# Row decays by DMA instead of matmuls, two output rows finished later, and the step sizes' chain ahead of a silu, in a one-core decoder-layer kernel

## The chip, the cores and the metric

The kernel runs on one core of a Trainium2 chip. A core has five engines that run side by side, each with its own instruction stream in a fixed order: PE (TensorE, matmuls; its weight loads are listed as PEld), DVE (VectorE), ACT (ScalarE), POOL (GpSimd) and SP (which here only issues DMAs). An instruction that waits holds up everything behind it on its engine. The metric is the device time of one execution in microseconds (us). Of this kernel three runs are given, and one further execution that the hardware profiler recorded.

## What is computed

One inference step of one decoder layer, for one prompt of 2048 tokens and 32 sample tokens that share the weights: a mixer of two halves (gated linear attention "GLA" and a Mamba-2 state space "SSD"), cross-attention to a memory of 256 tokens, and a SwiGLU feed-forward of width 2816, with model width 1024. All is fp32; each large fp32 product is made of three matmuls on operands split into a high and a low part.

The part that the change touches first is the SSD half. It has 8 heads and goes in chunks of tokens. With step sizes `dt` (a softplus) and a per-head rate `a_head` the reference computes per chunk

```
lc = jnp.cumsum(dtc * a_head, axis=1)
seg = lc[:, :, None, :] - lc[:, None, :, :]
decay = jnp.exp(jnp.where(causal, seg, -jnp.inf))
cb = jnp.einsum('bthn,bshn->btsh', cc, bc)
y = (jnp.einsum('btsh,bshp->bthp', cb * decay * dtc[:, None], xc) + ...
```

so for each head and each chunk a square matrix exp(lc[t] - lc[s]) is needed. With the source token s on the partitions, lc[s] is one number per partition, and lc[t] is a row that all 128 partitions must see: the "row decays".

## The kernel before

**Phase A (0 to about 840 us)** does projections, convolution, SSD and GLA in four blocks of 512 tokens (starting near 0, 250, 430 and 610 us). A block first makes the convolution features and one narrow projection (tile `sp`: step sizes and gate ranks), applies silu to the features (`xc`, L209/L210), and then makes, in this order, z (`tm(0)`), g (`tm(1)`), q and k, and v, each as a long run of PE matmuls at L135 to L137. Beside these runs go generators that stand in a queue `side` and are stepped between projection units: `decays()` (the softplus chain L155 to L171, `dA` L629, cumulative sums `lc` by two matmuls L632/L633), `gates()` (L659 to L679), and then the SSD chunks, four of 128 tokens in a block, each as `ssd_first(c)` and `ssd_second(c)`. A scheduler puts the instructions of this phase into each engine's stream by priorities, so the streams are not in the order of the code; they are fixed when the kernel is built.

Row decays before, for every block: `lc` is split into two parts (`hl`, L641/L642), transposed by four PE instructions (L646) and copied to 16 partitions of `sp` (`lcT`, L647). For each chunk POOL multiplies these 16 rows by a mask into a tile `R` of 16 x 1024 (L775), which was zeroed once in the block (L679). Two matmuls against a matrix of ones (`onesr`, L801), 128 x 512 each, put the rows onto all 128 partitions in PSUM. DVE takes min and difference with lc[s] from PSUM into `M` (L805, eight of 128 x 128 a chunk), ACT the exponential (L806), DVE multiplies by the masked C·B product (L809, two), and PE uses `M` as weights (L819, eight matmuls).

ACT keeps one table of functions at a time: silu and exp stand in different ones, and each change is an ACT_TABLE_LOAD in its stream. The code asks for the exponentials' table after the silus of the features, of z (L728) and of g (L735, L863).

**The passes behind (840 us to the end)** are the mixer's output, the scores, the value product, the feed-forward gate/up (kind "g", three units, the first starting near 1367 us) and down. Each is a row of units of seven products in a Strassen-like scheme with twelve matmul groups; the order of the code is kept. The seven products need sums of input pieces, which ACT (L1739) and DVE (L1743) prepare from tiles `st` that SP loads (L1795); the piece makers are called `now` (this unit) and `coming` (the next pass). Finished output rows are post-processed by generators in the list `posts`, each of which `tick()` advances by one step per product: `after_rows(j, m)` scales a row block (L1830), adds the residual by DMA, sums squares (L1900), scales by the root mean square into `u` (L1906), and `turned` transposes it on PE (L1863, eight). Row blocks are numbered (j, m) with j = 0 to 7 and m = 0, 1; the last two values of j finish when the value pass has ended and the gate/up pass has begun. Only when `posts` is empty in the gate/up pass does `leave_attention()` (L2178) free the attention's tiles and start the samples' work.

## Time and profile before

| | us |
|---|---|
| three runs | 2791.37, 2798.59, 2800.58 |
| their median | 2798.59 |
| the profiled execution, its own time | 2795.36 |
| its span (first to last recorded instruction) | 2793.6 |

| engine | busy us | share of the span |
|---|---|---|
| PE | 2720.1 | 97% |
| DVE | 2075.6 | 74% |
| ACT | 1472.2 | 53% |
| POOL | 540.1 | 19% |

The profile is one execution. A view by windows gives, per stretch of time, each engine's busy time with its number of instructions, the granted clock of PE (1.00 is full speed) and the DMA's share. A view of waits gives how long an engine stood idle, for which instruction and line, and which instruction of which other engine ended that. A timeline gives start and length of single instructions, with equal neighbours drawn together. PE's matmuls are pipelined: one begins before the one ahead has ended, so what a matmul costs is the distance from its start to the next start, and not its length.

### The profile page before, as it was taken

The page shows a single profiled execution, that of the slowest core. Times are in us where ns is not written, and L with a number is a line of the kernel's source. Part 1 is how long each engine was busy: PE and PEld are TensorE (multiplying, and loading weights), DVE is VectorE, ACT ScalarE, POOL GpSimd, SP SyncE. Part 2 cuts the span into 40 slices and gives each one's busy share as a digit, 9 for nine tenths or more (in the row PEclk, how much of TensorE's full clock was granted, in tenths as well). Part 3 has the DMA queues.
Part 4 walks back from the last instruction along what each step waited for, and adds up shares of the span by engine and source line. Part 5 has one row for each costly group of instructions (what it writes and reads, how often), then busy time and mean ns, then how long its engine had stood idle before and what let it go on. Part 6 is the DMA issues. An engine that isn't in the chain of part 4 may idle for free.

```text
span 2793.6 us, 41826 instructions
## 1 busy us (share of the span) xinstructions
PE 2720.1 (97%) x15207; PEld 2362.1 (85%) x15207; DVE 2075.6 (74%) x3831; ACT 1472.2 (53%) x2921; POOL 540.1 (19%) x722
## 2 busy tenths in 40 slices
PE   8999999999999999999899999999999999999998
PEld 8988888787886888888799888899999998788886
DVE  7676677776758787777888788668678888574776
ACT  5545554544547787777755434434445555353432
POOL 2142332321321321025321210001000001000011
PEclk9999999999999999999999999999999999999999
DMA  7345435343267885468764567775235436465765
GB/s 257 114 143 190 150 103 163 121 129 95 83 193 254 284 303 216 152 200 255 260 219 179 189 239 240 255 252 179 99 138 179 152 121 211 163 218 109 240 157 130
DMA packets 151102, 512.17 MB, mean 183 GB/s; under 512 B 18176, under 2 KB 29488, under 8 KB 137328
## 3 DMA queue, kind: packets, MB, share of 16 engines
q1 hardware_dynamic: 94560, 331.81, 36.3%
q0 software_dynamic: 44240, 152.82, 16.8%
q10 hardware_dynamic: 12096, 24.86, 2.7%
q8 instruction: 120, 1.97, 0.3%
q14 instruction: 86, 0.70, 0.1%
HBM read 365.76 MB, written 143.67 MB: 182 GB/s over the span
## 4 chain that ended last, share of the span: by engine, by line
PE 78%; DVE 11%; ACT 4%; issue 3%; DMA 3%; POOL 1%; DVEq 0%; POOLq 0%; SPq 0%; ACTq 0%
PE accA L135 10%; PE accA L136 10%; PE accA L137 10%; PE accC L135 5%; PE acc L135 5%; PE accC L137 5%; PE accC L136 5%; PE acc L136 5%; PE acc L137 5%; PE accB L135 3%; PE accB L137 3%; PE accB L136 3%; DVE s L1670 2%; DVE sum L1650 1%; PE mx L1863 1%
## 5 line engine op out<-in xcount | busy, mean ns | idle before, releaser
L135 PE MATMUL accA<-r,s 128*128 128x512 f32 (+2 forms) x1792 | 636.5, 355 | 17.4 <-ACT r L1739 5.8
L137 PE MATMUL accA<-r,s 128*128 128x512 f32 (+2 forms) x1792 | 629.0, 351 | 3.3 <-DVE s L1670 3.2
L136 PE MATMUL accA<-r,s 128*128 128x384 f32 (+2 forms) x1472 | 503.1, 342 | 3.1 <-DVE r L1743 3.0
L135 PEld LDWEIGHTS accA<-r,s 128*128 128x128 f32 x1792 | 339.6, 190 | 67.2 <-issue 9.7
L1668 ACT ACTIVATE s<-sum 128x512 fp32r<-128x512 f32 (+1 forms) x456 | 282.1, 619 | 192.6 <-DVE sum L1650 89.9
L137 PEld LDWEIGHTS accA<-r,s 128*128 128x128 f32 x1792 | 339.6, 189 | 33.8 <-DVE s L1670 4.7
L1670 DVE TENSOR_TENSOR s<-sum,s 128x512 fp32r<-128x512 f32 (+1 forms) x456 | 306.5, 679 | 20.5 <-ACT s L1668 20.1
L135 PE MATMUL accC<-r,s 128*128 128x512 f32 (+2 forms) x896 | 316.9, 354 | 4.4 <-ACT sg L1977 2.8
L137 PE MATMUL accC<-r,s 128*128 128x512 f32 (+2 forms) x896 | 312.6, 349 | 0.0
L136 PEld LDWEIGHTS accA<-r,s 128*128 128x128 f32 x1472 | 279.2, 190 | 20.8 <-DVE r L1743 5.1
L1670 DVE TENSOR_TENSOR s<-raw,s 128x512 fp32r<-128x512 f32 (+1 forms) x342 | 232.8, 681 | 51.3 <-ACT s L1668 50.3
L136 PE MATMUL accC<-r,s 128*128 128x384 f32 (+2 forms) x736 | 250.0, 340 | 0.5 <-DVE r L1743 0.5
L1668 ACT ACTIVATE s<-raw 128x512 fp32r<-128x512 f32 (+1 forms) x342 | 212.8, 623 | 66.3 <-PE accC L137 48.5
L129 ACT ACTIVATE whi<-wraw 128x1024 fp32r<-128x1024 f32 (+2 forms) x140 | 128.8, 934 | 184.7 <-PE acc L136 104.6
L135 PEld LDWEIGHTS accC<-r,s 128*128 128x128 f32 x896 | 168.6, 188 | 31.6 <-ACT sg L1977 6.3
L130 DVE TENSOR_TENSOR wlo<-wraw,whi 128x1024 fp32r<-128x1024 f32 (+2 forms) x140 | 152.3, 1099 | 47.2 <-ACT whi L129 46.5
L137 PEld LDWEIGHTS accC<-r,s 128*128 128x128 f32 x896 | 168.6, 188 | 14.7 <-DVE s L1670 0.2
L143 POOL TENSOR_TENSOR rs<-ms,nhalf 128x1 f32<-128x1 f32 (+4 forms) x125 | 113.0, 906 | 345.8 <-DVE ms L141 330.8
L135 PE MATMUL acc<-xhl,whi 128*128 128x512 f32 (+1 forms) x464 | 167.5, 362 | 8.4 <-ACT xhl L294 8.3
L137 PE MATMUL acc<-xhl,wlo 128*128 128x512 f32 (+1 forms) x464 | 163.6, 354 | 1.7 <-DVE wlo L130 1.7
L136 PE MATMUL acc<-xhl,whi 128*128 128x512 f32 (+1 forms) x464 | 163.5, 354 | 0.2 <-DVE xhl L295 0.2
L1650 DVE TENSOR_TENSOR sum<-raw 128x512 f32<-128x512 f32 (+1 forms) x228 | 157.4, 690 | 3.6
(696 smaller groups left out, 5854.6 us busy)
## 6 DMA issues: line engine op xcount, KB each, us to landing
raw<-in_w_gu_dram SPq DMA_DIRECT2D x66, 1024.0 KB, 4.9
wraw<-in_w_in_fm_dram SPq DMA_DIRECT2D x52, 512.0 KB, 3.7
wraw<-in_w_in_tm_dram SPq DMA_DIRECT2D x48, 512.0 KB, 4.0
st<-in_w_down_dram SPq DMA_DIRECT2D x37, 512.0 KB, 5.8
aT<-og POOLq DMA_DIRECT2D x22, 768.0 KB, 4.8
raw<-aT SPq DMA_DIRECT2D x16, 1024.0 KB, 6.3
out_y_dram<-y POOLq DMA_DIRECT2D x28, 512.0 KB, 6.0
yp<-y POOLq DMA_DIRECT2D x28, 512.0 KB, 6.6
```

Of the source, the lines that this page charges most:

```text
L129: last[0] = nc.scalar.activation(hi[:, cs], raw[:, cs], AF.Copy)
L130: nc.vector.tensor_tensor(lo[:, cs], raw[:, cs], f(hi)[:, cs], op=ALU.subtract)
L135: nc.tensor.matmul(ps, lhsT=wh, rhs=ah, start=start, stop=False, skip_group_check=more)
L136: nc.tensor.matmul(ps, lhsT=wh, rhs=al, start=False, stop=False, skip_group_check=more)
L137: nc.tensor.matmul(ps, lhsT=wl, rhs=ah, start=False, stop=stop, skip_group_check=more)
L143: nc.gpsimd.tensor_tensor(out=rs[:rows, :cols], in0=ms[:rows, :cols], in1=nhalf[:rows, :cols], op=ALU.pow)
L1650: nc.vector.tensor_tensor(t[out], x, y, op=o)
L1668: nc.scalar.activation(h3, v, AF.Copy)
L1670: return lambda: nc.vector.tensor_tensor(l3, v, f(h3), op=ALU.subtract)
L1863: nc.tensor.transpose(ps[kt // 4][:, kt % 4 * P:(kt % 4 + 1) * P], u[:, kt * P:(kt + 1) * P], ident)
```

## The change

Three edits.

1. **Row decays by DMA.** A third small matmul in `decays()` makes `lc` transposed at once (`dA` as weights, the triangle as moving operand, 32 x 128). ACT copies it to `lcT`, POOL issues a DMA of these 16 KB to a DRAM tile `lcD`, and for each chunk POOL issues a DMA that reads that chunk's eight rows (4 KB) once for each partition into a tile of 128 x 1024: `load_lc(c)`, into `M` for even chunks and into `R` for odd ones. Chunk 0's is issued in `decays()`, chunk c+1's at the start of `ssd_first(c)`. DVE's min and difference then work in place on that tile in SBUF. `R`'s builds on POOL and its zeroing, the two matmuls against ones of each chunk, the split, the four transposes and their copy are gone.
2. **Last value rows.** In `after_rows`, for the value rows of j = 6 and 7, a wait until the piece maker has nothing to prepare beside this product (`filling[0]` false), and then a pause of `7 * (j == 7) + 2 * m` products.
3. **silu moved.** The silu of the features stands behind the first step of `decays()` in the code, and no longer ahead of it.

```diff
@@ decays(), ssd_first()
-        silu(xc_[:, 0:4], xc_[:, 4:8])
         drain(side)
...
             nc.tensor.matmul(ps[:, 0:32], lhsT=triu, rhs=dA, start=True, stop=True)
             nc.tensor.matmul(ps[:, 32:64], lhsT=ones, rhs=dA, start=True, stop=True)
+            pt = mxt()
+            nc.tensor.matmul(pt[0:32, 0:P], lhsT=dA, rhs=triu, start=True, stop=True)
+            nc.scalar.copy(lcT, pt[0:32, 0:P])
+            nc.gpsimd.dma_start(out=lcD[b], in_=lcT)
...
+            load_lc(0)
             nc.scalar.activation(wl_, wl_, AF.Exp)
-            hl = pa.tile([P, NCH, 16], F32R, name="hl")
-            lc3 = lc.rearrange("p (c h) -> p c h", h=8)
-            nc.scalar.activation(hl[:, :, 0:8], lc3, AF.Copy)
-            nc.vector.tensor_tensor(hl[:, :, 8:16], lc3, f(hl)[:, :, 0:8], op=ALU.subtract)
-            yield
-            ps = mxt()
-            for c in range(NCH):
-                nc.tensor.transpose(ps[0:16, c * CH:(c + 1) * CH], f(hl)[:, c], ident)
-            nc.vector.tensor_copy(lcT, ps[0:16])
-            yield
-
+            yield
+
+        Ms = {}
+
+        def load_lc(c):
+
+            Ms[c] = pa.tile([P, 8, CH], F32, name="MR"[c % 2])
+            nc.gpsimd.dma_start(out=Ms[c].rearrange("p h t -> p (h t)"),
+                                in_=lcD[b, 8 * c:8 * c + 8].rearrange("h t -> (h t)").unsqueeze(0).broadcast_to([P, 8 * CH]))
...
-            Rs.append(pa.tile([P, 8, CH], F32R, name="R"))
-            nc.gpsimd.memset(f(Rs[0]), 0.0)
...
         side.append(decays())
         step(side)
+        silu(xc_[:, 0:4], xc_[:, 4:8])
         side.appendleft(gates())
...
-            R = Rs[0]
-            nc.gpsimd.tensor_tensor(out=R[64:80], in0=lcT[:, cs].unsqueeze(1).broadcast_to([16, 8, CH]),
-                                    in1=bmask[64:80].unsqueeze(2).broadcast_to([16, 8, CH]), op=ALU.mult)
-            M = pa.tile([P, 8, CH], F32, name="M")
+            M = Ms.pop(c)
+            if c + 1 < NCH:
+                load_lc(c + 1)
...
-            for g in range(2):
-                pl = mxt()
-                nc.tensor.matmul(pl, lhsT=onesr, rhs=R[:, 4 * g:4 * g + 4], start=True, stop=True)
-                plv = pl.rearrange("p (h t) -> p h t", t=CH)
-                for h in range(4):
-                    s1 = lc[:, c * 8 + 4 * g + h:c * 8 + 4 * g + h + 1]
-                    nc.vector.tensor_scalar(M[:, 4 * g + h], plv[:, h], s1, s1, op0=ALU.min, op1=ALU.subtract)
+            for h in range(8):
+                s1 = lc[:, c * 8 + h:c * 8 + h + 1]
+                nc.vector.tensor_scalar(M[:, h], M[:, h], s1, s1, op0=ALU.min, op1=ALU.subtract)
             nc.scalar.activation(M, M, AF.Exp)
@@ after_rows(), and the loop over products
+    filling = [False]
...
             nc.sync.dma_start(out=u, in_=x[rows(j, m)])
+        elif j + 2 >= NJ:
+            while filling[0]:
+                yield
+            yield from pause(7 * (j + 1 == NJ) + 2 * m)
         yield
...
         p = coming if work[cur][2] == 1 else now if begins[cur] else None
+        filling[0] = p is not None
```

In the streams of the built kernels the change shows at more places than the code. Lines of the changed kernel stand some three to nine lower than those of the one before; in names, the number behind the underscore tells one buffer from another, and what an instruction waits for stands in brackets.

**ACT, head of block 2** (the features' silu is L209, the softplus chain begins with Abs L158 and Exp L159, L659/L661 or L657/L659 copy gate ranks, L129 splits weights; then z's silus, L728 or L724, among the gates' exponentials L676/L677 or L674/L675). Before:

```order
L605 COPY sp_5153<-acc_5159 40x512 [waits PE_49]
L209 ACT_TABLE_LOAD
L209 ACTIVATE xc_4597<-xc_4597 128x2048
L209 ACTIVATE xc_4597<-xc_4597 128x2048 [waits DVE_49]
L210 ACT_TABLE_LOAD
L158 ACTIVATE spe_5195<-spx_5193 128x32 [waits DVE_49]
L659 ACTIVATE sps_244<-sp_5153 16x512
L159 ACTIVATE spe_5195<-spe_5195 128x32 [waits Activation_49]
```

Now:

```order
L604 COPY sp_5106<-acc_5112 40x512 [waits PE_49]
L129 ACTIVATE whi_5280<-wraw_5278 128x1024 [waits DMAHW1_49]
L657 ACTIVATE sps_242<-sp_5106 16x512 [waits DVE_49]
L659 ACTIVATE sps_242<-sp_5106 16x512
L158 ACTIVATE spe_5145<-spx_5143 128x32 [waits DVE_49]
L159 ACTIVATE spe_5145<-spe_5145 128x32 [waits Activation_49]
L209 ACT_TABLE_LOAD
L209 ACTIVATE xc_4550<-xc_4550 128x2048 x2
L210 ACT_TABLE_LOAD
```

The chain's two exponential steps went from behind the silu to ahead of it, with one weight split and both copies. Twenty rows further on, z before:

```order
L728 ACT_TABLE_LOAD
L728 ACTIVATE z_5390<-acc_5223 128x512 [waits PE_49]
L676 ACT_TABLE_LOAD [waits DVE_49]
L676 ACTIVATE bd_5187<-bd_5187 128x1024 [waits Activation_49]
L638 ACTIVATE wl__5183<-wl__5183 128x96 [waits DVE_49]
L677 ACTIVATE bd_5187<-bd_5187 128x1024 [waits Activation_49]
L641 ACTIVATE hl_5321<-lcl_5182 128x4x8
L728 ACT_TABLE_LOAD
L728 ACTIVATE z_5390<-acc_5224 128x512 [waits PE_49]
L728 ACTIVATE z_5390<-acc_5225 128x512 [waits PE_49]
L728 ACTIVATE z_5390<-acc_5226 128x512 [waits PE_49]
L735 ACT_TABLE_LOAD
```

and now:

```order
L724 ACT_TABLE_LOAD
L724 ACTIVATE z_5338<-acc_5176 128x512 [waits PE_49]
L674 ACT_TABLE_LOAD [waits DVE_49]
L674 ACTIVATE bd_5137<-bd_5137 128x1024 [waits Activation_49]
L724 ACT_TABLE_LOAD
L724 ACTIVATE z_5338<-acc_5177 128x512 [waits PE_49]
L675 ACT_TABLE_LOAD
L675 ACTIVATE bd_5137<-bd_5137 128x1024 [waits Activation_49]
L724 ACT_TABLE_LOAD
L724 ACTIVATE z_5338<-acc_5178 128x512 [waits PE_49]
L724 ACTIVATE z_5338<-acc_5179 128x512 [waits PE_49]
L731 ACT_TABLE_LOAD
```

Four table loads have become six here. Counted over the whole stream, block 0 keeps its 6 table loads, block 1 goes from 8 to 10, and blocks 2 and 3 go from 8 to 12 each.

**DVE, chunks of block 2** (`M` and `R` are the tiles of chunks 0/2 and 1/3, `xdt` the tokens scaled by their step sizes, which a chunk's L819 or L810 needs as well). Before, chunk 0:

```order
L647 COPY sp_5153<-mx_5354 16x512 [waits PE_49]
L783 TENSOR_TENSOR xdt_5403<-mx_5398,dt_5181 128x512 [waits PE_49]
L785 TENSOR_TENSOR xD_5405<-mx_5398,cols_88 128x512
L797 TENSOR_TENSOR cbm_5417<-mx_5414,triu_232 128x256 [waits PE_49]
L805 TENSOR_SCALAR M_5397<-mx_5419,lcl_5182 128x128 [waits PE_49]
L805 TENSOR_SCALAR M_5397<-mx_5419,lcl_5182 128x128 x3
L805 TENSOR_SCALAR M_5397<-mx_5425,lcl_5182 128x128 [waits PE_49]
L805 TENSOR_SCALAR M_5397<-mx_5425,lcl_5182 128x128 x3
```

Now, the stretch between the end of chunk 1 and chunk 2's last work:

```order
L814 TENSOR_TENSOR xD_5482<-mx_5550,xD_5482 128x512 [waits Pool_49]
L796 TENSOR_SCALAR R_5614<-R_5614,lcl_5132 128x128 [waits DMASW4_49]
L796 TENSOR_SCALAR R_5614<-R_5614,lcl_5132 128x128 x6
L141 TENSOR_SCALAR ms_5572<-ss_5569 128x2 [waits Activation_49]
L796 TENSOR_SCALAR R_5614<-R_5614,lcl_5132 128x128
L829 TENSOR_SCALAR z_5338<-z_5338,rs_5574 128x256 [waits Pool_49]
L829 TENSOR_SCALAR z_5338<-z_5338,rs_5574 128x256
L778 TENSOR_TENSOR xdt_5621<-mx_5616,dt_5131 128x512 [waits PE_49]
L780 TENSOR_TENSOR xD_5623<-mx_5616,cols_88 128x512 [waits DVE_49]
L792 TENSOR_TENSOR cbm_5635<-mx_5632,triu_231 128x256 [waits PE_49]
L800 TENSOR_TENSOR M_5473<-M_5473,cbm_5635 128x512 [waits DVE_49]
```

The min and difference no longer wait for PE; they wait for their chunk's load, and chunk 3's stand ahead of chunk 2's `xdt`, `cbm` and product. POOL's stream around it:

```order
L646 DMA M_5473<-lcD_253 128x1024 [waits DMASW1_49,DVE_49,DMASW3_49,PE_49,Activation_49]
L816 TENSOR_TENSOR z_5338<-xD_5353,z_5338 128x512 [waits DVE_49]
L143 TENSOR_TENSOR rs_5439<-ms_5437,nhalf_86 128x2 [waits DVE_49]
L782 TENSOR_TENSOR xw_5484<-xdt_5480,wl__5133 128x512 [waits DVE_49,Pool_49]
L646 DMA R_5614<-lcD_253 128x1024 [waits DVE_49,DMASW2_49,PE_49,Activation_49]
L813 TENSOR_TENSOR xD_5482<-xD_5482,y_5559 128x512 [waits DVE_49,Pool_49]
```

The load of chunk 3 (R_5614) waits for PE's last use of chunk 1's tile, and POOL's `xD` sum of chunk 1 stands behind it.

**PE, where the value pass meets the gate/up pass** (`u` holds a finished row block that L1863 or L1856 transposes; L135 to L137 are the products). Before:

```order
L135 MATMUL accA_13489<-r0_13002,s_13387 128x384
L136 MATMUL accA_13489<-r0_13002,s_13387 128x384
L137 MATMUL accA_13489<-r0_13002,s_13387 128x384
L1863 MATMUL mx_13509<-ident_77,u_13464 128x128 [waits PE_49,Activation_49]
L1863 MATMUL mx_13509<-ident_77,u_13464 128x128 x3
L1863 MATMUL mx_13510<-ident_77,u_13464 128x128 x4
L135 MATMUL accA_13297<-r2_13452,s_13415 128x384 [waits DVE_49,Activation_49]
L136 MATMUL accA_13297<-r2_13452,s_13415 128x384 [waits DVE_49]
```

Now, 145 rows further down:

```order
L135 MATMUL accA_13661<-r0_12909,s_13580 128x384
L136 MATMUL accA_13661<-r0_12909,s_13580 128x384
L137 MATMUL accA_13661<-r0_12909,s_13580 128x384
L1856 MATMUL mx_13681<-ident_77,u_13639 128x128 [waits Activation_49]
L1856 MATMUL mx_13681<-ident_77,u_13639 128x128 x3
L1856 MATMUL mx_13682<-ident_77,u_13639 128x128 x4
L135 MATMUL accA_13500<-r2_13325,s_13609 128x384 [waits DVE_49]
L136 MATMUL accA_13500<-r2_13325,s_13609 128x384
```

With the gate/up pass beginning at product 169 of the passes behind phase A, the transposes of row (6, 1) went from product 174 to 188, those of (7, 0) from 186 to 201 and those of (7, 1) from 188 to 203; those of (6, 0) stay at 171.

9 lines of the change are left out of this document (3 added, 6 removed).

## The prediction

> **What bounds the kernel now.** I read the page first, then the chain of waits, then windows of the stage that changes, then what PE waits for there.
>
> ```profile
> span 2793.6 us, 41826 instructions
> PE 2720.1 (97%) x15207; PEld 2362.1 (85%) x15207; DVE 2075.6 (74%) x3831; ACT 1472.2 (53%) x2921; POOL 540.1 (19%) x722
> PE 78%; DVE 11%; ACT 4%; issue 3%; DMA 3%; POOL 1%; DVEq 0%; POOLq 0%; SPq 0%; ACTq 0%
> ```
>
> PE is busy for 97% of the span and holds 78% of the chain that ended last. Below, the first row is blocks 1 to 3 of phase A, the second the passage from the value pass to gate/up, the third a stretch inside the first gate/up unit (busy time of PE, PEld, DVE, ACT, POOL, then the granted clock, the DMA's share, GB/s).
>
> ```profile
> 240.00:840.00 600.00, 589.92 (x3140) 480.96 (x3138) 417.81 (x854) 295.83 (x576) 172.93 (x200) 1.00 0.43 134
> ...
> 1360.00:1380.00 20.00, 18.25 (x88) 16.34 (x88) 16.10 (x28) 16.10 (x34) 5.77 (x9) 0.83 0.71 233
> ...
> 1440.00:1460.00 20.00, 20.00 (x117) 19.87 (x115) 19.45 (x60) 10.45 (x23) 2.72 (x5) 1.00 0.48 176
> ```
>
> In blocks 1 to 3 PE is idle for 10.1 of 600 us at full clock, so a matmul taken out there is time saved nearly whole, while DVE (70%), ACT (49%) and POOL (29%) have room. The passage at 1360 is the one place here with a low clock (0.83). PE's waits in phase A, ranked:
>
> ```profile
> PE mx L819 <- DVE M L809: 3.0, 4, 1.3
> PE mx L801 <- POOL R L775: 2.8, 3, 1.0
> PE mx L632 <- DVE dA L629: 2.6, 3, 0.9
> ```
>
> These (us in total, times, longest) are the decays' own path: `dA` late, POOL's `R` late, the finished matrix late.
>
> **Edit 1, PE's work.** In block 2, chunk 0:
>
> ```profile
> 536.36 0.41 PE L632 MATMUL mx<-dA,triu 128*128 128x32 f32 x2 [0.86 <-DVE dA L629]
> 536.61 0.39 PE L633 MATMUL mx<-dA,ones 128*128 128x32 f32 x2
> ...
> 539.41 0.60 PE L646 MATMUL mx<-ident,hl 128*16 128x128 f32 x4
> 539.85 0.60 PE L781 MATMUL mx<-ident,xc 128*128 128x128 f32 x4
> ...
> 542.83 0.50 PE L801 MATMUL mx<-R,onesr 128*128 128x512 f32 x1 [0.86 <-POOL R L775]
> 543.16 0.39 PE L135 MATMUL acc<-whi,xhl 128*128 128x512 f32 x1
> 543.40 0.40 PE L801 MATMUL mx<-R,onesr 128*128 128x512 f32 x1
> 543.63 0.39 PE L136 MATMUL acc<-wlo,xhl 128*128 128x512 f32 x1
> ```
>
> By start to next start the two L801 take 0.33 and 0.23, mean 0.28; over 32 of them 9.0 (bounds: all at 0.23 or all at 0.33, so 7.4 to 10.6). The four transposes take 539.85 - 539.41 = 0.44 a block, over four blocks 1.8. The new matmul is not in the trace. From below it costs as much as L632, 536.61 - 536.36 = 0.25 for its two passes; its moving operand is 128 wide like four transposes of 0.11 each, so 0.44 bounds it from above. It lies nearest L632, so 4 x 0.25 = 1.0 (to 1.8). **PE's work: -9.0 - 1.8 + 1.0 = -9.8** (-7.4 to -11.4).
>
> **Edits 1 and 3, the waits removed.** POOL's `R` is no longer on the path, so 2.8 falls. `dA` is late for the reason that ACT's rows show:
>
> ```profile
> 513.90 1.28 ACT L209 ACT_TABLE_LOAD   x1
> 515.19 3.72 ACT L209 ACTIVATE xc<-xc 128x2048 f32<-128x2048 f32 x2
> ...
> 520.23 0.23 ACT L158 ACTIVATE spe<-spx 128x32 f32<-128x32 f32 x1
> 520.36 0.61 ACT L659 ACTIVATE sps<-sp 16x512 fp32r<-16x512 f32 x1
> ...
> 521.77 1.06 ACT L129 ACTIVATE whi<-wraw 128x1024 fp32r<-128x1024 f32 x1
> ```
>
> The chain's Abs stands 520.23 - 513.90 = 6.3 us behind the start of the silu's first table load, and the silu moves behind it. In the changed stream one weight split (1.06) and two copies (0.61) come before, so Abs gains about 4 us and the silu is late by about 3. Its reader, the transposes L781, comes at 539.85, twenty us after the silu's end (515.19 + 3.72), which covers that. The changed PE stream asks for `dA` 24 matmuls behind the gates' matmuls where it was 55; the 31 between, at the 0.23 of 543.40 to 543.63, are 7.1 us, more than Abs gains, but DVE's part of the chain, which before lies spread among other work until 536.3, is drawn together in the new order. I take both: 2.6 + 2.8 = **-5.4** (bounds: -2.8 if the wait for `dA` stays whole, and -5.4).
>
> **Edit 1, what replaces it.** ACT's copy of 32 x 128, POOL's write of 16 KB and its reads of 512 KB. The nearest rows of a write and of a read:
>
> ```profile
> xps<-sx POOLq DMA_DIRECT2D x7, 32.0 KB, 2.1
> ...
> z<-in_w_xo_dram POOLq DMA_DIRECT2D x8, 512.0 KB, 5.0
> ```
>
> and, of one row sent to all partitions (the gain rows `ga`, 4 KB read 128 times, which is the shape of the new load), with what POOL needs to issue a DMA:
>
> ```profile
> DMA to landing us min/median/max: 3.0/6.5/9.4
> ...
> 92.47 0.54 POOL L412 DMA_DIRECT2D kv<-kraw  x1 [5.02 <-DVE spx L155]
> ```
>
> For chunk 0: 2.1 + 6.5 and two issues of 0.54 make 9.7 us from `lcT`, some 11 from the matmul. PE needs chunk 0's product 90 stream rows behind, about 20 us, and DVE has 5 to 7 us of work between the load and it (fourteen L796, `xdt` to `cbm` and the products, at the prices below): covered, by 2 to 4. Chunk 3's load is the tightest, because it may start only when PE has finished chunk 1, which uses the same tile, and chunk 3's min and difference stand on DVE ahead of chunk 2's last work. PE and DVE there before:
>
> ```profile
> 564.65 1.89 PE L819 MATMUL mx<-xdt,M 128*128 128x64 f32 x16
> ...
> 581.23 1.89 PE L819 MATMUL mx<-xdt,M 128*128 128x64 f32 x16
> ...
> 534.38 0.28 DVE L918 TENSOR_SCALAR Sp<-Sg,em 128x128 f32<-128x128 f32 x1
> ...
> 568.85 0.68 DVE L831 TENSOR_TENSOR Ss<-Ss,mx 128x512 f32<-128x512 f32 x1
> ...
> 572.33 0.62 DVE L838 TENSOR_SCALAR z<-z,rs 128x256 f32<-128x256 f32 x2 [0.82 <-POOL rs L143]
> ...
> 574.94 2.63 DVE L805 TENSOR_SCALAR M<-mx,lcl 128x128 f32<-128x128 f32 x8
> ...
> 578.76 1.29 DVE L809 TENSOR_TENSOR M<-M,cbm 128x512 f32<-128x512 f32 x2
> ```
>
> Issued near 566.5 the load lands at 573.0 with 6.5. DVE reaches L796 at 569.5 and stands idle 3.5 us. PE wants chunk 2's product at 581.2. Between the two DVE has eight L796 at 0.28 (L918 is the same operation from SBUF; 2.63 / 8 = 0.33 is the price from PSUM), 2.2; z's scaling to `cbm`, 574.94 - 572.33 = 2.6; the products, 1.3: 6.1. So **the load may take 581.2 - 6.1 - 566.5 = 8.6 us**: 6.5 passes, 9.4 does not. I count one late load in each block and 0.6 for it, 2.4, against half of the M wait of 3.0, which the step from POOL to PE that is gone gives back: **+1** (from -3.0, all of that wait gone and no load late, to +12, 0.75 lost by each of 16 loads).
>
> **Edit 3, table loads.** The changed ACT stream has ten more, 2 + 4 + 4 in blocks 1 to 3: z's and g's silus now alternate with exponentials. Each is 1.28 (513.90 above), and 513.90 + 1.28 = 515.18 is when the silu starts, so nothing is added behind one. It costs PE time only where a PSUM bank of z or g is emptied later than the next projection wants it; the changed PE stream fills the two banks emptied first and goes on with them before it asks for the other two, and ACT is half idle there. Of 12.8 I take **+1.5** (0 to 12.8). The Trainium skill, "ScalarE: Activation LUTs", section "What ACT_TABLE_LOAD costs", speaks against this edit more strongly: it gives about 1.38 us of drain behind each load, 2.66 us for a switch, 26.6 for ten as an estimate. This trace shows no such gap behind a load; the row decides.
>
> **Edit 2.** In the passage PE stands still here:
>
> ```profile
> 1360.62 0.80 PE L135 MATMUL accA<-r,s 128*128 128x512 f32 x1 [3.84 <-DVE y L1850]
> ...
> 1376.81 1.09 PE L1863 MATMUL mx<-ident,u 128*128 128x128 f32 x8 [1.12 <-ACT u L1906]
> ...
> 1380.78 0.45 PE L135 MATMUL accA<-r,s 128*128 128x384 f32 x1 [0.79 <-ACT r L1739]
> 1383.02 0.44 PE L136 MATMUL accA<-r,s 128*128 128x384 f32 x1 [1.80 <-DVE r L1743]
> ```
>
> The 3.84 is of the pass's own input and the move does not touch it. The other three, 3.7 us, are row (6, 1) itself (1.12) and input sums that ACT and DVE reach late. The window's clock of 0.83 costs 0.17 x 18.25 = 3.1 more; half of it, 1.6, I put to these three, the rest to the 3.84. With row (6, 1) and the scaling of (7, 0) gone 14 products later, 1.12 goes surely. But the same DVE work of three rows (1.27 to scale one, as its median says) comes where DVE is at 19.45 of 20:
>
> ```profile
> L1830 DVE SCALAR_TENSOR_TENSOR y<-y,rs,ga x46: 1274/1277/1286, 880.2 to 2772.8; 128x1024 f32<-128x1024 f32 x46
> ```
>
> Taken: **-2.5**, about half of 5.3 (from -5.3 to +3.8, three scalings on the path). Leaving the attention 15 products later costs nothing by itself while the samples' work still fits into the gate/up pass.
>
> **The sum**: -9.8 - 5.4 + 1 + 1.5 - 2.5 = -15.2. The profiled execution took 2795.36 (2793.6 of span and 1.8 around), which gives 2780.2; the three runs' median lies 3.2 above it, which gives 2783.4. Forecast **2782**.
>
> **The rivals.** (a) *Gains eaten on ACT*: z's and g's banks are emptied behind the ten loads and PE waits for them, 12.8 in place of 1.5, so 2793. For it: the added loads stand directly ahead of the silus that empty those banks; against: PE's waits in phase A name no silu of z or g before. (b) *The moved rows collide*: 0 to +3.8 in place of -2.5, so 2785 to 2788, with DVE at 97% for it and the three short waits against. (c) *The load is late*, the slower case: where it takes longer than 8.6 us DVE stops at chunk 3's L796, with chunk 2's product behind it; chunk 0, with chunk 1's L796 ahead of its own `xdt`, is alike, so there are eight places. At twice the median, 13, they lose 4.4 each, 35 in all: 2817. The forecast's whole gain of 16 is gone from 8.6 + 16 / 8 = 10.6 us on. For it: loads of 9.4 exist; against: the DMAs are 43% busy in blocks 1 to 3. A variant is that DVE's own work in SBUF, 2.2 us a chunk, holds back a load that POOL is issuing: 6.5 + 2.2 = 8.7 is just at the bound, 9.4 + 2.2 = 11.6 would cost 3.0 x 8 = 24, 2806. I give it 0.02 of the chance of (c). POOL's writes land no later than SP's loads of the same size, which speaks against it:
>
> ```profile
> st<-in_w_down_dram SPq DMA_DIRECT2D x37, 512.0 KB, 5.8
> ...
> out_y_dram<-y POOLq DMA_DIRECT2D x28, 512.0 KB, 6.0
> ```
>
> The Trainium skill, "SBUF — State Buffer", section "SBUF: two separate sides", states that variant as a rule: a DVE operation in a two-port mode keeps GpSimd from writing the descriptors of its DMAs. No run shown here has such an operation beside a load to all partitions. (d) *The change does less than it says*: of four rows of edit 2 only (6, 1) leaves the passage, and if its place is taken by another late sum the edit is worth 0: 2784.5. (e) *More than forecast*: all waits gone, 9.8 + 5.6 + 3.0 + 5.3 = 23.7: 2772 to 2775.
>
> **How the numbers follow.** Forecast with (d) 0.58, (b) 0.14, (a) 0.17, (c) 0.06, (e) 0.05. Own range of the forecast 2774 to 2790. The range for 8 in 10 takes in (e), (b) and (a), and the runs' own spread of 9 us: 2767 to 2797. About 0.3% (8.4 us) is what a measurement of this kernel tells from no change. Faster by more, below 2790.2: the forecast, (b) and (e) nearly whole, 0.76; within: (a) and the edge of the others, 0.18; slower: (c), 0.06.
>
> **What would show it.** Right: PE's busy time in phase A 9 to 10 us less, no PE wait for `dA` or POOL, DVE idle for 2 to 4 us before the min and difference of chunk 3, ended by a DMA, and PE's wait for the product of L800 at most what it was; the row of (6, 1) without its 1.12. Wrong: PE idle for ACT's z or g, loads landing after more than 8.6 us, or a gate/up unit with more idle PE than now. The sum fails if phase A ends less than 10 us earlier.

## The result, and the profile after

The changed kernel takes 2770.27 us (median of four runs, 2766.88 to 2773.92), the kernel before 2794.98 (four runs, 2788.59 to 2800.58). The ratio is 0.9913, with a 95% interval of 0.99 to 0.9926: 24.7 us faster. The forecast was 2782 with a range of 2767 to 2797, and faster was the likeliest case. So the direction and the wide range held. The size did not: 2770 lies below the forecast's own range of 2774 to 2790.

The profiled execution took 2773.92 us. The page's first lines:

```profile
span 2772.2 us, 41723 instructions
...
PE 2705.8 (98%) x15167; PEld 2355.2 (85%) x15167; DVE 2062.0 (74%) x3821; ACT 1483.9 (54%) x2931; POOL 520.2 (19%) x722
```

The span is 21.4 us shorter than before's 2793.6. To see where, I cut both spans at the same matmuls and take a window of each piece. Columns: the window, its length, busy time of PE, PEld, DVE, ACT and POOL with the number of instructions, the granted clock, the DMA's share, GB/s. The pieces are phase A (less its last 7.5 us), the passage from the value pass to gate/up, the first gate/up unit with what follows it, and two stretches behind. Before:

```profile
0.00:840.00 840.00, 816.75 (x4710) 687.99 (x4710) 590.30 (x1200) 417.81 (x793) 244.27 (x295) 1.00 0.46 146
1331.30:1461.00 129.70, 122.15 (x658) 115.08 (x657) 109.94 (x225) 84.33 (x178) 42.49 (x63) 0.96 0.71 238
1461.00:1584.90 123.90, 119.42 (x746) 110.33 (x745) 101.34 (x220) 64.75 (x118) 24.47 (x32) 1.00 0.55 193
1584.90:1874.50 289.60, 284.41 (x1792) 256.09 (x1792) 221.14 (x394) 123.08 (x229) 23.90 (x39) 0.99 0.70 242
1874.50:2037.00 162.50, 162.50 (x950) 157.59 (x949) 120.03 (x207) 71.68 (x139) 14.78 (x24) 1.00 0.40 138
```

After:

```profile
0.00:825.50 825.50, 806.43 (x4670) 681.37 (x4670) 576.86 (x1190) 430.02 (x803) 223.84 (x295) 1.00 0.49 159
1317.60:1443.60 126.00, 120.28 (x658) 114.10 (x657) 100.97 (x172) 82.90 (x176) 35.31 (x52) 0.97 0.64 212
1443.60:1558.90 115.30, 114.34 (x690) 108.39 (x689) 101.59 (x245) 57.98 (x108) 23.46 (x31) 1.00 0.58 203
1558.90:1850.70 291.80, 284.48 (x1800) 257.90 (x1798) 228.44 (x419) 131.54 (x245) 32.64 (x51) 0.99 0.71 241
1850.70:2017.40 166.70, 166.70 (x1006) 158.96 (x999) 121.09 (x211) 71.38 (x138) 14.88 (x24) 1.00 0.46 160
```

| piece | before us | after us | difference us | PE's matmuls |
|---|---|---|---|---|
| phase A | 840.0 | 825.5 | -14.5 | 4710 to 4670 |
| between | 491.3 | 492.1 | +0.8 | |
| passage | 129.7 | 126.0 | -3.7 | 658, the same |
| first gate/up unit | 123.9 | 115.3 | -8.6 | 746 to 690 |
| next stretch | 289.6 | 291.8 | +2.2 | 1792 to 1800 |
| the one behind | 162.5 | 166.7 | +4.2 | 950 to 1006 |
| the rest | 756.6 | 754.8 | -1.8 | |
| sum | 2793.6 | 2772.2 | -21.4 | |

Two things stand out. Phase A is 14.5 shorter: PE's busy time falls by 10.3 (816.75 to 806.43) and its idle time by 4.2. And the first gate/up unit, of which the forecast says only that idle PE there would speak against it, gives 8.6. It has 56 matmuls fewer (work for the sample tokens), and the two stretches behind it have more (8 and 56 by these windows, which count a matmul at an edge in both). The work moved: of the 8.6, 5.1 is busy time (119.42 to 114.34) and 3.5 is PE's idle time, 4.5 before and 1.0 now.

PE's waits in phase A after (us in total, times, longest):

```profile
PE acc L135 <- ACT xhl L294: 9.0, 1, 9.0
PE mx L752 <- DVE z L829: 2.2, 2, 2.0
PE acc L135 <- ACT fold L458: 1.8, 2, 1.1
```

The first was there before (8.3). The waits for `dA` (2.6), for POOL's `R` (2.8) and for the finished `M` (3.0) are all gone. In their place stand z's scaling (0.5 before, 2.2 now) and the `fold` of L458 (not in the list before, 1.8 now).

### The profile page after: what moved, and what is told of

Its sections match the earlier page's. It is cut to its first block, busy times and chain, and to the rows that moved or that the text cites. A ratio compares the mean times of both kernels' runs of the same rounds, so it can differ in the third digit from the quotient of the medians.

```text
span 2772.2 us, 41723 instructions
## 1 busy us (share of the span) xinstructions
PE 2705.8 (98%) x15167; PEld 2355.2 (85%) x15167; DVE 2062.0 (74%) x3821; ACT 1483.9 (54%) x2931; POOL 520.2 (19%) x722
## 5 line engine op out<-in xcount | busy, mean ns | idle before, releaser
L135 PE MATMUL accA<-r,s 128*128 128x512 f32 (+2 forms) x1792 | 633.7, 354 | 13.8 <-DVE t L1999 4.7
L137 PE MATMUL accA<-r,s 128*128 128x512 f32 (+2 forms) x1792 | 626.3, 350 | 1.2 <-DVE s L1661 1.1
L135 PEld LDWEIGHTS accA<-r,s 128*128 128x128 f32 x1792 | 338.4, 189 | 61.5 <-issue 7.5
L137 PEld LDWEIGHTS accA<-r,s 128*128 128x128 f32 x1792 | 338.0, 189 | 30.6 <-DVE s L1661 1.9
L135 PE MATMUL accC<-r,s 128*128 128x512 f32 (+2 forms) x896 | 318.9, 356 | 7.2 <-ACT sg L1974 5.0
L137 PE MATMUL accC<-r,s 128*128 128x512 f32 (+2 forms) x896 | 314.2, 351 | 0.0
L129 ACT ACTIVATE whi<-wraw 128x1024 fp32r<-128x1024 f32 (+2 forms) x140 | 128.4, 933 | 187.7 <-PE acc L136 106.2
L135 PEld LDWEIGHTS accC<-r,s 128*128 128x128 f32 x896 | 169.6, 189 | 34.2 <-ACT sg L1974 8.7
L137 PEld LDWEIGHTS accC<-r,s 128*128 128x128 f32 x896 | 169.8, 190 | 14.8 <-DVE s L1661 0.2
L135 PE MATMUL acc<-xhl,whi 128*128 128x512 f32 (+1 forms) x464 | 167.9, 363 | 9.2 <-ACT xhl L294 9.0
L137 PE MATMUL acc<-xhl,wlo 128*128 128x512 f32 (+1 forms) x464 | 163.4, 353 | 1.7 <-DVE wlo L130 1.7
```

The source lines that it names most:

```text
L129: last[0] = nc.scalar.activation(hi[:, cs], raw[:, cs], AF.Copy)
L135: nc.tensor.matmul(ps, lhsT=wh, rhs=ah, start=start, stop=False, skip_group_check=more)
L137: nc.tensor.matmul(ps, lhsT=wl, rhs=ah, start=False, stop=stop, skip_group_check=more)
```

## The experiments

The kernel before ran in every group of runs: medians 2794.67 (20 runs), 2795.23 (16) and 2795.0 (9).

| kernel | what it has | median us | ratio, 95% interval |
|---|---|---|---|
| e1 | edit 1 | 2780.99 | 0.9946, 0.9934 to 0.9958 |
| e2 | edits 1 and 3 | 2777.54 | 0.9935, 0.9923 to 0.9947 |
| e3 | edit 2 | 2789.0 | 0.998, 0.9971 to 0.9989 |
| e4 | edit 3 | 2787.65 | 0.9977, 0.9967 to 0.9987 |
| e5 | edits 1 and 3, late leave | 2774.23 | 0.9922, 0.9909 to 0.9934 |
| e6 | all three, load in small pieces | 2781.32 | 0.995, 0.9936 to 0.9963 |
| e7 | all three, 35 more table loads | 2786.06 | 0.9968, 0.9956 to 0.998 |
| e8 | before, one residual add later | 2796.39 | 1.0004, 0.9995 to 1.0014 |
| e9 | all three, again | 2772.85 | 0.9915, 0.9898 to 0.9932 |
| e10 | edits 1 and 2 | 2777.28 | 0.9926, 0.9907 to 0.9945 |
| e11 | all three, later leave still | 2784.2 | 0.9955, 0.9939 to 0.9972 |

The difference of two medians is uncertain by some 3 us (the intervals), so small differences need more than the times. The profiled executions help, when each is cut at the same products: phase A up to the first product of the passes behind it, then the passage, the first gate/up unit and all that lies behind phase A (us; smallest to largest where a row has several executions).

| edits in phase A | profiles of | phase A |
|---|---|---|
| none | before, e3, e8 | 847.6 to 851.1 |
| 3 | e4 | 843.5 |
| 1 | e1, e10 | 833.5 and 838.2 |
| 1 and 3 | after, e2, e5, e9, e11 | 830.1 to 833.0 |

| edit behind phase A | profiles of | passage | first unit | all behind phase A |
|---|---|---|---|---|
| none | before, e1, e2, e4, e8 | 126.6 to 129.8 | 123.7 to 126.9 | 1945.3 to 1947.4 |
| 2 | after, e3, e6, e7, e9, e10 | 122.9 to 126.0 | 115.4 in all | 1935.9 to 1940.6 |
| late leave | e5 | 127.1 | 114.7 | 1935.8 |
| 2, later leave still | e11 | 125.4 | 111.9 | 1948.6 |

The same code differs by up to 5 us from one execution to the next; the groups do not overlap, though some only just.

### Edit 1 alone (e1)

```diff
  (against the changed kernel)
+        silu(xc_[:, 0:4], xc_[:, 4:8])
         drain(side)
...
         step(side)
-        silu(xc_[:, 0:4], xc_[:, 4:8])
...
-        elif j + 2 >= NJ:
-            while filling[0]:
-                yield
-            yield from pause(7 * (j + 1 == NJ) + 2 * m)
```

> Edit 1 alone: the decays go by DMA, but the features' silu stays ahead of the softplus chain and the value rows are finished as before. Theory A (the load needs the early chain): PE's work falls by 10.3 us and the waits for POOL's R (2.8) go, but dA's matmul now stands 47 stream rows (10.7 us) ahead of chunk 0's product instead of 91, while the way over DRAM took about 11 us in the changed kernel (write 3.9, load 5.4, two issues) with 5 to 7 us of DVE work behind it: some 5 to 7 us of waiting in each of blocks 1 to 3, so in all -13 + 15 to 21 = +2 to +8 against the kernel before, with waits of PE for the product of L802 as its mark. Theory B (edit 3 only removes the wait for dA, the load is covered anyway): -12 (the whole gain of phase A, 14.5, without dA's 2.6).

Measured: 13.7 us faster, close to theory B. PE's waits in phase A, two rows of them:

```profile
PE mx L629 <- DVE dA L626: 2.7, 3, 1.0
PE mx L811 <- issue: 2.2, 3, 0.9
```

The wait for `dA` stays whole with this edit, and the wait for `R` is gone with its cause. For the second row the view of waits names no waker. The timeline of block 2 has one:

```profile
535.86 2.14 DVE L797 TENSOR_SCALAR M<-M,lcl 128x128 f32<-128x128 f32 x8 [2.00 <-DMA M<-lcD]
...
540.35 1.08 PE L811 MATMUL mx<-xdt,M 128*128 128x64 f32 x8 [0.82 <-issue]
```

DVE stands idle for 2.00 us until chunk 0's load has landed, and the first half of its product (L801) ends at 540.25, 0.1 us before PE begins. So the mark of theory A is there in each of the three blocks, but it costs 2.2 us in all where 15 to 21 were expected. From the `dA` matmul to PE's product pass 13.1 us (527.25 to 540.35), and the load has landed 8.6 us into them; the write took 1.7 us here and not 3.9.

### Edits 1 and 3 (e2), and edits 1 and 2 (e10)

e2 is e1 with the silu where the changed kernel has it; e10 is the changed kernel with the silu put back:

```diff
  (e10, against the changed kernel)
+        silu(xc_[:, 0:4], xc_[:, 4:8])
         drain(side)
...
         step(side)
-        silu(xc_[:, 0:4], xc_[:, 4:8])
```

> Edits 1 and 3 without edit 2: the value rows are finished as before. Theory A (the parts add up by place): phase A's 14.5 us and nothing else, -14 to -16 against the kernel before; the passage from the value pass to gate/up keeps its waits of 3.8, 1.1, 0.8 and 1.8. Theory B (what the passage gained came from phase A ending at another moment relative to the DMAs, not from the moved rows): -18 to -21, and the 3.8 wait is smaller here too.

> Edits 1 and 2 without edit 3 (the silu back ahead of the softplus chain). Theory A (what edit 3 gains inside the changed kernel is the wait for dA, 2.7, and the 2.2 before the product, less four more table loads and one late z): 2 to 5 us above the changed kernel. Theory B (edit 3's 7 us, measured on the kernel before, come on top): 6 to 8 us above it.

Measured: e2 is 17.1 faster than before, 3.4 more than e1; e10 is 4.4 slower than the changed kernel in the same group, as its theory A has it (2777.28 to 2772.85; in both pairs the intervals of the ratios overlap). For e2 the 17.1 lies between its two theories: PE's wait of 3.8 in the passage is smaller here too (1.5), as theory B has it, but what lies behind phase A is as long as before (1945.3 beside 1946.0), so that the gain is phase A's, as in theory A. e10 has both of e1's waits back:

```profile
PE mx L629 <- DVE dA L626: 2.7, 3, 0.9
PE mx L811 <- issue: 2.2, 3, 0.8
```

So beside edit 1, edit 3 is worth about 3.4 to 4.4 by the medians, and these two waits (4.9) are gone with it.

### Edit 3 alone (e4)

```diff
  (against the kernel before)
-        silu(xc_[:, 0:4], xc_[:, 4:8])
         drain(side)
...
         side.append(decays())
         step(side)
+        silu(xc_[:, 0:4], xc_[:, 4:8])
```

> Edit 3 alone on the kernel before: the silu of the features behind the softplus chain's first step, two more table loads instead of ten. Theory A: the wait for dA (2.6) goes, nothing else, -2 to -3. Theory B (the shift of the silu by about 3 us or the table loads cost something): 0 to +3.

Measured: 7.0 faster, where 2 to 3 was expected. The waits of e4 in phase A show why, by what they lack and by two rows:

```profile
PE mx L800 <- DVE xD L784: 3.0, 3, 1.6
...
PE mx L818 <- DVE M L808: 0.5, 1, 0.5
```

No wait for `dA` is left, no wait for POOL's `R`, and of `M`'s 3.0 only 0.5; one of 3.0 behind `xD`, which the list of before has not, takes part of it back (e3, with the phase A of before, has 1.6 of that wait too). The whole chain of the decays was late because its first step was late. With the silu out of its way, POOL's `R` is in time too. So the waits for `R` and `M` belong to edits 1 and 3 both: either edit takes most of them away, and together they cannot take them twice. The parts (13.7, 5.7, 7.0) do add up to more (26.4) than the changed kernel gains in any group of runs (22.2 to 24.7), but with some 3 us of uncertainty in each the times alone would not show it; the lists of waits do.

### Edit 2 alone (e3), and the late leave (e5)

e3 is the kernel before with the lines of edit 2. e5 has edits 1 and 3, leaves the value rows as before, and only holds `leave_attention()`, and with it the samples' work, for 15 products more (the expectation counts 16):

```diff
  (e5, against e2)
+    held_off = [0]
...
         if samp2 is None and k == XG and not posts:
-            leave_attention()
+            held_off[0] += 1
+            if held_off[0] > 15:
+                leave_attention()
```

> Edit 2 alone on the kernel before. Theory A: the passage's 5.3 us and what follows, -5 to -8. Theory B (the passage's gain was an accident of DMA timing): between -3 and +1, with the 3.8 wait of PE for the input sums still there.

> Edits 1 and 3 with the value rows finished as before, but the attention left (and the samples' work begun) 16 products later. Theory A (edit 2's gain comes from the samples' work starting later, behind the first gate/up unit's crowded stretch): 4 to 6 us below the kernel with edits 1 and 3 alone, that is -21 to -23 against the kernel before, and PE's waits of the first unit for DVE's L1670 (1.6 to 3.0 us) and for the samples' ge (1.3) gone as in the changed kernel. Theory B (the gain comes from the rows' own work leaving the passage): -16 to -18, as edits 1 and 3 alone, and those waits still there.

Measured: e3 is 5.7 faster than before, as its theory A has it. e5 is 21.0 faster than before, as its theory A has it; it comes to 2774.23, beside 2770.27 and 2772.85 of the changed kernel, without moving one row. PE's waits in e5's first gate/up unit are a single row:

```profile
PE mx L1212 <- DVE sBm L1209: 0.5, 1, 0.5
```

In e2, which leaves at the old time, the same stretch has these:

```profile
PE accA L137 <- DVE s L1661: 2.8, 1, 2.8
PE mx L1253 <- DVE ge L1246: 1.3, 1, 1.3
```

So e5 gains 3.9 over e2 (21.0 less 17.1), and the changed kernel 5.1 to 7.6; these intervals overlap, but the second table above does not leave it open. With the late leave alone the first unit is as short as with edit 2 (114.7 and 115.4, not 123.7 to 126.9), while the passage stays as it was: most of edit 2's gain comes from the late start of the samples' work. How that work holds up the first unit stands in DVE's stream in e2:

```profile
1528.66 0.69 DVE L1218 TENSOR_TENSOR Ms<-Ms,mx 128x512 f32<-128x512 f32 x1 [4.63 <-POOL Ms L1213]
```

A sum of the samples' state (`Ms`) waits 4.63 us for POOL, and the unit's own sums `s`, which PE waits for, stand behind it on DVE. In before the same step waits 3.42, in the changed kernel 0.9, in e5 it does not wait for POOL at all.

### The leave later still (e11)

```diff
  (against the changed kernel)
-            leave_attention()
+            held_off[0] += 1
+            if held_off[0] > 10:
+                leave_attention()
```

> The changed kernel with the attention left another 11 products later. Theory A (the samples' first work only has to miss the first unit's crowded stretch, which it does already): within 2 us of the changed kernel. Theory B (later is better still, because the waits of 4.6 us around products 3100 to 3700 of the matmuls are of the same kind): 2 to 5 us below it. If the samples' work no longer fits into the gate/up pass, it is slower by what is drained at the end.

Measured: 2784.2, 11.4 slower than the changed kernel in the same group, which neither theory gave. The first unit is shorter still (111.9), but the two stretches behind it, 292.1 and 166.5 in the changed kernel, take 300.9 and 170.9. PE's waits there, in the stretch that answers to the end of the samples' work:

```profile
PE mx L1340 <- DMA sraw<-in_w_out_dram: 5.3, 1, 5.3
PE accA L135 <- DVE t L2000: 3.2, 2, 1.7
```

The first of them is a load of the samples' own weights. So the delay has a limit not far behind where the changed kernel stands: 10 products more (the expectation counts 11) cost half of its whole gain.

### The passage: one residual add later (e8)

The forecast took the 3.84 us wait for a fact of the pass's own input. In the kernel before, the row (6, 0) residual add (a 512 KB DMA `y<-hX`, issued by POOL at 1346.19) goes 0.23 us ahead of the load of that input (`st`, issued by SP at 1346.42). In the changed kernel the `st` load was issued ahead of the add. The view of the tile `st` from 1344 to 1357 us before, and from 1330 to 1345 us after, has from issue to landing (smallest, median, largest):

```profile
DMA to landing us min/median/max: 7.0/8.1/8.8
```

```profile
DMA to landing us min/median/max: 3.4/7.1/9.4
```

The load in question took 8.8 before and 3.4 after. The experiment issues the add one product later, in the kernel before:

```diff
  (against the kernel before)
+            if (j, m) == (NJ - 2, 0):
+                yield
             add_rows(y, hX[rows(j, m)])
-            yield from pause(6)
+            yield from pause(5 if (j, m) == (NJ - 2, 0) else 6)
```

> The kernel before with one step moved: the residual add of value row (6, 0) is issued one product later on POOL, so behind the load of the input sums that PE waits for (3.84 us in the profile of before, where the add was issued 0.23 us ahead of that load and the load took 8.8 us; 3.6 us in the kernels in which it is issued 1 us behind it). Theory A (that order of two DMAs makes the wait): the load lands in 3.5 to 5 us, the wait falls to 1.3 to 1.9, the time by 2 to 4. Theory B (the load's length is a matter of the DMAs' general crowding): wait and time as before, within 1 us.

Measured: the load takes 4.2 where it took 8.8, and the 3.84 falls to 1.49, so the add just ahead of the load does cause it. But the time stays (1.0004, interval 0.9995 to 1.0014). PE's waits in e8's passage:

```profile
PE accA L135 <- ACT sg L1979: 3.5, 1, 3.5
PE accA L135 <- DVE y L1850: 1.5, 1, 1.5
PE mx L1863 <- ACT u L1908: 1.2, 1, 1.2
```

A wait of 3.5 for `sg`, which before's passage has not, stands in its place. What follows is that a shorter wait was no gain by itself here: the next late thing is right behind it. e1 and e2 say the same: the load goes ahead of the add in them too, the wait is 1.5, and what lies behind phase A is as long as before.

### More table loads (e7)

```diff
  (against the changed kernel, behind each of the silus of z and g but the last)
+                if i < 3:
+                    tc.keep_in_program_order(nc.scalar.preload_act_table_set("natural_log_exp_and_others"))
```

> The changed kernel with the exponentials' table asked for after each of z's and g's silus: 90 table loads in ACT's stream instead of 55, 35 more at 1.28 us, 45 us on ACT. Theory A (the loads lie beside PE's work, ACT is half idle): less than 0.2 us each, 0 to +7. Theory B (they keep PSUM banks from PE): half or more of their time, +22 to +45. Against the kernel before: -24 to -17 (A), about 0 to +20 (B).

Measured: 2786.06, 13 to 16 us slower than the changed kernel's two medians. ACT has 90 table loads instead of 55 (the largest group of them, in the view by lines: count, busy time, mean ns, idle time ahead):

```profile
L724 ACT ACT_TABLE_LOAD x32 | 41.1, 1283 | 0.3
```

The added loads stand in phase A, which takes 847.9 us here (830.1 to 833.0 without them). PE's waits there have grown where z is late:

```profile
PE mx L754 <- DVE z L831: 6.1, 3, 4.2
...
PE acc L135 <- ACT fold L458: 3.5, 1, 3.5
```

35 added loads cost 13 to 16 us, about 0.4 each, in between what the two theories gave. The Trainium skill, "ScalarE: Activation LUTs", section "What ACT_TABLE_LOAD costs", has 2.66 us for a switch, some 93 for 35 as an estimate. The runs have less than a fifth of that: most of a load of 1.28 lies beside PE's work.

### The load in small pieces (e6)

To reach the bound of 8.6 us, the row was read in pieces of 128 bytes:

```diff
  (against the changed kernel)
-    lcD = tc.dram_tile([NB, 32, P], F32, name="lcD")
+    lcD = tc.dram_tile([NB, 32, 4, 64], F32, name="lcD")
...
-            nc.gpsimd.dma_start(out=lcD[b], in_=lcT)
+            nc.gpsimd.dma_start(out=lcD[b][:, :, 0:32], in_=lcT.rearrange("h (q t) -> h q t", t=32))
...
-                in_=lcD[b, 8 * c:8 * c + 8].rearrange("h t -> (h t)").unsqueeze(0).broadcast_to([P, 8 * CH]))
+                in_=lcD[b, 8 * c:8 * c + 8].rearrange("h q t -> (h q) t")[:, 0:32].unsqueeze(0).broadcast_to([P, 32, 32]))
```

> The changed kernel with each load of the row decays cut into 32 pieces of 128 bytes a partition instead of one of 4 KB, so that it lands later; no other work is added. The prediction's bound: in block 2 of the changed kernel chunk 3's load took 5.0 us, DVE stood 2.4 us for it and chunk 2's product was ready 2.1 us early, so up to about 7.1 us it costs nothing and beyond that PE waits for the product of L800 by what the load is longer, at two to four places a block. With a landing of 10 us: 3 us x 12 = +25 to +36 against the changed kernel, if of 15 us: +60 or more. Theory B (the load is not on the path, DVE finds other work): less than +5 at any landing.

Measured: 2781.32, some 8 to 11 slower than the changed kernel, but the landings are only a little longer, 5.5 to 8.4 us for `R`:

```profile
DMA to landing us min/median/max: 5.5/6.8/8.4
```

POOL needs 1.7 us to issue such a load instead of 0.57. The scheduler also built other streams for the longer issue (51 table loads, not 55, and a weight split ahead of `y` on DVE), and PE waits 7.3 us for z's scaling in two places, where the changed kernel has 2.2. So, as far as these views go, the price is not that of the landing alone, and the run does not decide what a load beyond 8.6 us costs.

### The changed kernel again (e9)

A plain repeat beside e10 and e11:

> The changed kernel itself, on the same chip as the two beside it, to compare with them and to see which waits of its first profile come back. All theories: -22 to -27 against the kernel before; the wait of 2.0 us for block 1's last z and none for dA, POOL or the finished matrix again in phase A.

Measured: 2772.85, ratio 0.9915, and the waits of the profile after show again, z's among them:

```profile
PE mx L752 <- DVE z L829: 2.1, 2, 1.7
```

No version that was run has a lower median than the changed kernel.

## Why the prediction was right and where it was wrong

The time lies inside the stated range and the direction is right, so the forecast holds; its sum was too small. Of the 11.7 us between 2782 and 2770.27, 3.6 come from the median before, which the fourth run took from 2798.59 to 2794.98, and 8.1 from the gain. Against the profiled execution the sum said -15.2, and the spans show -21.4. The 6.2 between them split by place: phase A 1.8 (-12.7 said, -14.5 measured), the passage and the samples' work 3.4 (-2.5 said; -3.7 - 8.6 + 2.2 + 4.2 = -5.9 measured), and 1.0 in the rest, which the forecast had at nothing.

By the first table of the experiments this pair is a modest one for phase A: over all profiles its gain is 14.6 to 21.0.

**PE's work: right.** -9.8 said, -10.3 measured. The number of matmuls agrees with the count of the edit: 32 of L801 and 16 transposes less, 8 passes of the new one more, 40 in all. In block 2 the new matmul (L630) takes 521.18 - 520.84 = 0.34 where 0.25 was taken and 0.44 the bound:

```profile
520.84 0.41 PE L630 MATMUL mx<-triu,dA 128*32 128x128 f32 x2
521.18 0.50 PE L135 MATMUL acc<-whi,xhl 128*128 128x512 f32 x1
```

**The waits for `dA` and `R`: right in size, wrong in their cause.** Both are gone, -5.4. But the step put 2.8 to edit 1 alone and 2.6 to edit 3, and e4 shows that edit 3 without edit 1 removes both. With all three edits this makes no difference to the sum; of a change of one edit it would have forecast less than half (2 to 3 against 7.0).

**The loads: the mechanism was right, the term +1 was mis-sized.** It was a late load of 0.6 in each block against half of the wait for `M`. DVE does stand idle for chunk 3's load, as foretold, for 2.39 us where 3.5 was worked out, and PE asks for chunk 2's product only at 572.10:

```profile
563.58 1.89 DVE L796 TENSOR_SCALAR R<-R,lcl 128x128 f32<-128x128 f32 x7 [2.39 <-DMA R<-lcD]
...
568.58 1.37 DVE L800 TENSOR_TENSOR M<-M,cbm 128x512 f32<-128x512 f32 x2
```

```profile
572.10 1.89 PE L810 MATMUL mx<-xdt,M 128*128 128x64 f32 x16
```

DVE's product ends at 569.95, 2.15 before PE wants it. No load is late and the whole 3.0 of the `M` wait is gone: the term is -3.0, which was the end of its range. The load of chunk 3 was taken at 6.5 from `ga`'s row; those of the new rows in `R`, from block 1 on, land in 4.1 to 7.1, so that the 8.6 was never touched:

```profile
DMA to landing us min/median/max: 4.1/5.6/7.1
```

The 16 KB write, in return, was taken too short: 2.1 said; in block 1, for one, it took 3.9, beside 5.4 of the loads:

```profile
lcD<-lcT POOLq DMA_DIRECT2D x1, 16.0 KB, 3.9
...
M<-lcD POOLq DMA_DIRECT2D x2, 512.0 KB, 5.4
```

It cost PE no wait, since chunk 0's cover was longer than that.

**The table loads: too small, and put to the wrong edit.** The ten loads were put to edit 3. The streams have 45 loads before, 51 with edit 1 alone, 47 with edit 3 alone and 55 with both, so six of the ten come with edit 1. As to the price, +1.5 was taken; at e7's 0.4 for each the ten would be about 4. That no gap stands behind a load was right, in the changed stream too:

```profile
532.62 1.28 ACT L724 ACT_TABLE_LOAD   x1
533.91 0.60 ACT L724 ACTIVATE z<-acc 128x512 f32<-128x512 f32 x1
```

Part of the price of the ten is probably in the 2.2 of z's scaling and the 1.8 of `fold`, which stand in the list of waits now. That is argued from e7, where the same two grow; it is not shown for the ten loads themselves.

Phase A's terms after the fact are -10.3 of work, -8.4 of waits removed (2.6 + 2.8 + 3.0) and +4.2 of waits added (z's scaling 1.7, `fold` 1.8, the start's `xhl` 0.7), together -14.5. The last of these is no effect of the edits: that wait lies between 7.6 and 9.0 in all profiles, whatever the kernel.

**Edit 2: the wrong place and the wrong reason.** -2.5 was said, all of it in the passage. Three steps failed there. "With row (6, 1) ... gone 14 products later, 1.12 goes surely": PE's waits in the passage after are

```profile
PE mx L1856 <- ACT u L1903: 3.0, 1, 3.0
PE accA L135 <- DVE y L1843: 1.3, 1, 1.3
PE accA L136 <- DVE r L1734: 0.9, 1, 0.9
PE accA L135 <- ACT sg L1974: 0.5, 1, 0.5
```

and the first of them is the old 1.12, grown to 3.0 (the same 3.0 stands in e1, e2, e4 and e5, so it is no work of edit 2). It belongs to row (6, 0), which hardly moves, and not to (6, 1); I had read the transposes' row without following which row block they turn. "The 3.84 is of the pass's own input and the move does not touch it": the wait falls to 1.3. That it comes from the order of two DMAs is shown by e8; it falls in e1 and e2 as well (to 1.5, without edit 2), while in e4 the add still goes first, so the order changes with edit 1. In the kernels with the new order POOL stands 1.17 us ahead of the add for DVE's `y` (L1843), which it does not before; why it waits there is not settled, and e6, which has edit 1 too, has the old order. And "leaving the attention 15 products later costs nothing by itself": true, and it should have been priced as a gain. e5 shows that this delay alone brings most of what edit 2 brings, by keeping the samples' sums off DVE in the first unit. Besides, half of the price of the low clock did not belong to these three waits: the clock of before in that window is 0.50 from 1360 to 1365, 0.83 from 1365 to 1370 and 1.00 from 1370 to 1380, all of it behind the 3.84, while the first of the three begins at 1375.7. Edit 2 does shorten the passage (122.9 to 126.0 against 126.6 to 129.8), but not by the waits that were named; that it comes near -2.5 is luck.

**The rivals.** (a), gains eaten on ACT: at ten loads its sign, a PE wait for z's silu itself, is there with 0.4 us and no more, while e7 shows the mechanism at 45 (1.2 for that wait, 6.1 for z's scaling). (b), the moved rows collide: they do not; DVE's busy time in the passage falls from 109.94 to 100.97. (c), the late load: not reached, and its variant neither seen nor tested. Only three loads, in e7, are issued beside a min and difference, and only beside the last 0.1 us of one; they landed in 4.0 to 4.1 us, among the shortest of that run. What the traces do show is the reverse, a price that the sum left out. A min and difference in place in SBUF takes 0.34 us by the median, but where it begins while POOL works on a tile of 128 x 512, it ends only some 0.1 us after POOL does. In e1:

```profile
544.06 1.21 DVE L797 TENSOR_SCALAR R<-R,lcl 128x128 f32<-128x128 f32 x1
```

Such operations of 0.9 to 1.3 us stand in e1 and e10 three times each and in e7 seven times. In the changed kernel only the last 0.35 us of three POOL operations meet one, and it takes 0.43. In before, which reads PSUM there, 85 begin while POOL works and none takes over 0.41. The rule behind the variant (the Trainium skill, "SBUF — State Buffer", section "SBUF: two separate sides") is that an operation of DVE in a two-port mode and one of POOL shut each other out, for the whole of the one that began first. These rows agree with it for POOL's work on tiles, though no run shows which mode DVE was in; for the issue of a DMA no run shows it. (d), less than it says: not on the whole, though what it names (another late sum in the place of a removed wait) is what happens in the passage and in e8. (e), all waits gone and 23.7 in all, was given 0.05 and is nearest in time. It is right in phase A, but for the passage it is right by accident: its 5.3 are not the waits that went. Its 5.6 for `dA` and `R` is a slip for 5.4, so that it comes to 23.5.

**The marks.** PE's busy time 9 to 10 less (10.3), no wait for `dA` or POOL, DVE idle for 2 to 4 us ended by a DMA (2.39), phase A over 10 earlier (14.5): all there. The row without its 1.12: not there. Of the marks of being wrong, PE idle for z's silu is there with the 0.4 us named above.

**Still open**: what a load beyond 8.6 us costs, the ten table loads' own price, and why POOL's add waits for DVE in most kernels with edit 1.

## What to carry to other kernels

A chain's waits at several places may have one cause at its head: before putting each wait to the edit that touches its line, ask which of them would go if only the head came earlier. An edit that delays one thing also delays all that hangs on its end (here the samples' work, by an empty list of generators), and that can be the larger part, for better or worse. And a short wait on the path in a crowded stretch may be worth nothing: ask first what is late next behind it.

## What the runs showed of the hardware that was not expected

A DMA can be slowed by one issued just ahead of it on another queue. In before, e3, e4 and e6 POOL's add of 512 KB goes 0.23 to 0.25 us ahead of SP's load of 512 KB (`st`), and the load takes 8.8, 7.3, 6.7 and 4.4 us. In the eight profiles in which the add follows about 0.96 us behind, it takes 3.4 to 3.8, and in e8, with the add 3.9 us behind, 4.2. What the two share is not shown.

A DVE operation in place in SBUF that begins beside POOL's work can last until that ends, 1.21 us for 0.34 (the row of e1 at 544.06 above); of the 85 that read PSUM beside POOL's work in before none was held up so.

A short wait of PE can halve its clock for a while after. Behind the wait of 1.98 us for z's scaling in block 1 the granted clock is 0.50 from about 421 to 424 us:

```profile
419.00:420.00 1.00, 0.19 (x2) 0.22 (x3) 0.69 (x3) 0.53 (x3) 0.27 (x1) 1.00 0.00 0
420.00:421.00 1.00, 1.00 (x7) 0.87 (x6) 0.00 (x1) 1.00 (x2) 0.92 (x1) 0.93 0.51 184
421.00:422.00 1.00, 1.00 (x4) 0.74 (x3) 0.87 (x3) 0.88 (x4) 0.09 (x1) 0.50 0.78 311
422.00:423.00 1.00, 1.00 (x4) 0.81 (x3) 1.00 (x3) 0.00 (x0) 0.16 (x1) 0.50 0.07 29
423.00:424.00 1.00, 1.00 (x3) 0.76 (x3) 1.00 (x3) 0.00 (x0) 0.45 (x1) 0.50 0.94 367
424.00:425.00 1.00, 1.00 (x5) 0.82 (x4) 0.69 (x3) 0.00 (x0) 0.68 (x2) 0.87 1.59 334
```

By these rows 0.07 + 3 x 0.50 + 0.13 = 1.7 us of full clock are lost, nearly as much again as the wait itself, so such a wait can cost about twice what the list of waits says. It does not always: behind a wait of 2.12 us at 2080.30 of the same trace, and behind one of 3.01 at 1359.35 of e9, the clock stays at 1.00. The Trainium skill, "TensorE: Matmul & The Clock Gate", section "Part 1: The HAM clock gate (the "warmup" mystery)", has the clock fall after an idle window of about 3.4 us and come back after a busy one of the same length. The half-clock stretch here, (1 - 0.93) / 0.5 + 3 + (1 - 0.87) / 0.5 = 3.4 us, agrees with that length; but here some 2 us of idle PE were enough to start it.
